# Sums of weight quadrants by accumulating transfers in a seven-product feed-forward block

## The chip, the core and the metric

One Trainium2 chip, one of its cores. TensorE multiplies, VectorE and ScalarE (ACT) work on tiles, GpSimd (POOL) does small work, SyncE (SP) issues transfers, and 16 DMA engines carry them. The metric is device time in microseconds (us) of one execution; lower is better.

## The reference, cut to what matters

One layer of a streaming encoder over 512 rows of 1024 features: a feed-forward block, a mixer with three kinds of attention, a second feed-forward block, a final norm. The change touches the two feed-forward blocks alone, which are of one form (`D_FF` is 2816, all in float32):

```python
def swiglu(h, wg, wu, wd):
    return (jax.nn.silu(h @ wg) * (h @ wu)) @ wd

x = x + 0.5 * swiglu(rmsnorm(x, ffn1_norm[l]), ffn1_wg[l], ffn1_wu[l], ffn1_wd[l])
...
x = x + 0.5 * swiglu(rmsnorm(x, ffn2_norm[l]), ffn2_wg[l], ffn2_wu[l], ffn2_wd[l])
```

## The kernel before

Every float32 product is made of three matmuls of split operands: a tile is split into a high part (a cast by ACT, line 77) and a low part (a subtraction by VectorE, line 78), and high x high, high x low and low x high are summed.

The up products of a feed-forward block are computed by a scheme with seven products of quarter size in place of eight (the Strassen-Winograd scheme). A pair of feature tiles is an `Item`; there are 11 per block, 22 in the kernel. Its weights are a 2 by 2 grid of quadrants of 128 x 1024 words (512 KB): quadrants 0 and 1 are the first feature tile with the first and the second half of the contraction, 2 and 3 the second feature tile with the same. In one quadrant the columns of gate and of up weights stand side by side. The moving operands are the matching seven matrices `M[1]` to `M[7]`, made once per block by `Operands.combine` (lines 205 to 231) from the transposed, normalised rows: `t1` to `t4` are sums of quarters of those, held in buffers from `quarter()`, and each is split into `M[5]`, `M[6]`, `M[7]`, `M[4]`.

`Item.prep(p)` (line 371) gives the weight block of product p. Products 1, 2 and 4 use a quadrant as it was loaded (`raw`, a buffer out of six under the tag `raw`, loaded by the SP queue at line 98). The other four use sums of quadrants, which VectorE makes: s1 (line 379, product 5), s2 (line 380, product 6), s4 (line 385, product 3) and s3 (line 389, product 7). Sums lie in `quarter()` buffers: two tags, `kx` and `w4`, taken in turn, two buffers each. A new block begins with `t1` to `t4` in all four of them, so its first sums take the buffers that those leave. `block` then splits the raw tile or sum into one of six slots (four `whi`/`wlo`, two `fhi`/`flo`).

`Item.run(p, blk)` (line 418) multiplies: 24 matmuls of 128 x 256 columns (`mm7`, line 354), into three PSUM banks: `y` (tag `s`, two buffers) collects products 1, 6, 7 and 4, `z` (tags `p` and `o` in turn) collects 5 and 3, product 2 has a bank of tag `g`. Between them `snap` (line 397) copies what `y` holds so far to SBUF by ACT, after products 1, 6 and 7; `plus` adds such a copy to another bank; `gated` (line 405) makes silu(gate) x up.

The jobs go through `run_jobs` (line 320), which calls `prep` up to six blocks ahead of `run`. The code lists an item's jobs as 6, 5, 7, the next item's 1, then 4, 3 and the next item's 2. A scheduler sets the order on every engine from this, by what is ready in its own simulation; on TensorE, parts of jobs can be mixed. The first block handles 4 feature tiles (two items), then three times 6 (three items) per feed-forward block; after each such chunk its down product is run (`wd`, lines 110 to 112), and its first job comes ahead of the last item's 4 and 3. The first chunk starts with 1 and 2 of both of its items.

Of the kernel before, what the change touches and what calls it, by code (L numbers as in the profile page):

```python
# [41 lines left out]
HS = S // 2  # L42
# [5 lines left out]
def layer_kernel(ctx: ExitStack, tc: tile.TileContext, a: dict, out: bass.AP):  # L48
# [128 lines left out]
    def quarter():  # L177

        quarters[0] += 1
        return base.tile([P, 1024], F32, tag=("w4", "kx")[quarters[0] % 2], name="quarter", bufs=2)  # L180
# [4 lines left out]
    class Operands:  # L185
# [18 lines left out]

        def combine(self, t):
            M, (r0, r1) = self.M, self.raw
            sub = nc.vector.tensor_tensor
            cols, first = slice(t * P, (t + 1) * P), slice(t % 2 * P, (t % 2 + 1) * P)

            def part(i, raw, c):  # L210
                split(raw, M[i][0][:, :, c], M[i][1][:, :, c])

            if t < 2:
                part(1, r0[:, :, cols], cols)
                part(2, r1[:, :, cols], cols)
                return
            if t == 2:
                self.t1, self.t2 = k4(quarter()), k4(quarter())
            t1, t2 = self.t1, self.t2
            sub(out=t1[:, :, first], in0=r0[:, :, cols], in1=r0[:, :, first], op=ALU.subtract)  # L220
            sub(out=t2[:, :, first], in0=r1[:, :, cols], in1=t1[:, :, first], op=ALU.subtract)
            part(6, t2[:, :, first], first)
            if t == 3:
                lo, hi = slice(0, HS), slice(HS, S)
                split(t1, *M[5])
                t3, t4 = k4(quarter()), k4(quarter())
                sub(out=t3, in0=r1[:, :, hi], in1=r0[:, :, hi], op=ALU.subtract)
                split(t3, *M[7])
                sub(out=t4, in0=r1[:, :, lo], in1=t2, op=ALU.subtract)
                split(t4, *M[4])  # L230
                split(r1[:, :, hi], *M[3])

# [99 lines left out]
    def ffn(pre, x_sb, M, fp, after, raws=None, before_last=None, after_half=None):  # L332
# [24 lines left out]
        class Item:  # L357


            def __init__(self, ft, G, g0, raws):  # L360
                self.ft, self.G, self.g0 = ft, G, g0
                self.raws = list(raws or [])
                self.pr = [None, None]

            def raw(self, i):
                while len(self.raws) <= i:
                    n = len(self.raws)
                    self.raws.append(load(w1[self.ft + n // 2, n % 2], 1024))
                return self.raws[i]

            def prep(self, p):
                add = nc.vector.tensor_tensor
                if p == 1:
                    return block(self.raw(0))
                if p == 2:
                    return block(self.raw(1))
                if p == 6:
                    self.s1, self.s2 = quarter(), quarter()
                    add(out=self.s1, in0=self.raw(2), in1=self.raw(3), op=ALU.add)
                    add(out=self.s2, in0=self.s1, in1=self.raw(0), op=ALU.subtract)  # L380
                    return block(self.s2)
                if p == 5:
                    got = block(self.s1)
                    self.s4 = quarter()
                    add(out=self.s4, in0=self.raw(1), in1=self.s2, op=ALU.subtract)
                    return got
                if p == 7:
                    s3 = quarter()
                    add(out=s3, in0=self.raw(0), in1=self.raw(2), op=ALU.subtract)
                    return block(s3)  # L390
                if p == 4:
                    return block(self.raw(3))
                return block(self.s4)

            def snap(self):
                v = fp.tile([P, 512], F32, tag="snap", name="snap", bufs=3)
# [5 lines left out]
                nc.vector.tensor_tensor(out=c, in0=ps, in1=v, op=ALU.add)  # L402
                return c

            def gated(self, c, f, th):

                if self.pr[f] is None:
                    self.pr[f] = fp.tile([P, S], F32, tag="pr", name="pr", bufs=3)
                    self.n = 0
                sg = fp.tile([P, HS], F32, tag="sg", name="sg", bufs=2)  # L410
                nc.scalar.activation(out=sg, in_=c[:, :HS], func=AF.Silu)
                pr, cols = self.pr[f], slice(th * HS, (th + 1) * HS)
                nc.vector.tensor_tensor(out=pr[:, cols], in0=sg, in1=c[:, HS:], op=ALU.mult)

            def done(self, f):
                split(self.pr[f], *(v[:, self.g0 + f, :] for v in self.G))
# [1 line left out]
            def run(self, p, blk):  # L418
                if p == 1:
                    self.y = bank("s")  # L420
                    mm7(self.y, blk, 1, True)
                    self.p1 = self.snap()
                elif p == 2:
                    x = bank("g")
                    mm7(x, blk, 2, True)
                    self.gated(self.plus(x, self.p1), 0, 0)
                elif p == 6:
                    mm7(self.y, blk, 6, False)
                    self.u2 = self.snap()
                elif p == 5:  # L430
                    self.z = bank("p" if self.ft // 2 % 2 else "o")
                    mm7(self.z, blk, 5, True)
                elif p == 7:
                    mm7(self.y, blk, 7, False)
                    self.u3 = self.snap()
                    self.gated(self.plus(self.z, self.u3), 1, 1)
                elif p == 4:
                    mm7(self.y, blk, 4, False)
                    self.gated(self.y, 1, 0)
                    self.done(1)  # L440
                else:
                    mm7(self.z, blk, 3, False)
                    self.gated(self.plus(self.z, self.u2), 0, 1)
                    self.done(0)
# [5 lines left out]
        for n, nf in enumerate(CHUNKS):  # L450
# [8 lines left out]
            else:  # L459
                order += [(items[0], 1), (items[0], 2)]  # L460
            for i, item in enumerate(items):
                order += [(item, 6), (item, 5), (item, 7)]
                if i + 1 < len(items) and not (ft == 0 and i == 0):
                    order += [(items[i + 1], 1)]
                if ft == 0 and i == 0:
                    order += [(item, 4), (item, 3)]
                elif i + 1 < len(items):
                    order += [(item, 4), (item, 3), (items[i + 1], 2)]
# [659 lines left out]
```

## Time and profile before

| | |
|---|---|
| median of 3 runs | 1273.12 us (1272.8 to 1274.1) |
| the profiled execution, its own time | 1273.05 us |
| its span in the profile | 1271.3 us |
| first feed-forward block | about 0 to 372 us |
| second feed-forward block | about 914 us to the end |
| busy: TensorE / VectorE / ACT / POOL | 97% / 66% / 47% / 8% |

Rows of the trace name an instruction by engine, line and operation, with what it writes and reads. PE is TensorE's matmul, PEld its weight load, which overlaps; DVE is VectorE; SPq is the SP queue that issues transfers. "Idle" is the time for which the engine stood still just before an instruction, and the arrow names what ended it. An engine's idle time costs something only where the chain of work that ends last passes through it. Matmuls are pipelined, so that each is shown longer (0.28 us) than the 0.114 us after which the next begins.

### The profile page before, as it was taken

To read this page: it belongs to the slowest core of one execution; us is meant where nothing else is said; L and a number is where in the kernel's file an instruction comes from. 1 tells how busy PE (TensorE), PEld (TensorE's weight loads), DVE (VectorE), ACT (ScalarE), POOL (GpSimd) and SP (SyncE) were. 2 spreads that over 40 slices of the span, in tenths; PEclk is the share of its full clock that TensorE was granted. 3 is DMA by queue.
4 is the path that set the end of the run, shared out by engine and by line. 5 is a ranking of instruction groups with operands and counts; after the bars stand their busy time and mean duration, and the time that the engine had idled before them with its cause. 6 is when DMAs were issued, how large, how long until landed. Compare 5 with 4: busy or idle time off the path is not lost.

```text
span 1271.3 us, 19657 instructions
## 1 busy us (share of the span) xinstructions
PE 1232.4 (97%) x7808; PEld 1116.9 (88%) x7808; DVE 842.8 (66%) x1377; ACT 596.8 (47%) x1115; POOL 107.1 (8%) x108
## 2 busy tenths in 40 slices
PE   7799999999998999999999999999979999999997
PEld 7789989989986799999999999888878998998996
DVE  7977667667564756766765565453697766766753
ACT  7535425435443446554555454443463452543543
POOL 1100000000000301111221121020000000000002
PEclk8899999999999899999999999999989999999999
DMA  5533324322334403321222320254133242342311
GB/s 215 174 108 116 115 71 128 113 91 101 116 118 130 109 28 108 88 67 58 88 87 70 89 83 31 75 159 160 34 127 122 76 133 91 101 129 73 130 35 67
DMA packets 53084, 127.57 MB, mean 100 GB/s; under 512 B 10112, under 2 KB 10624, under 8 KB 52992
## 3 DMA queue, kind: packets, MB, share of 16 engines
q1 hardware_dynamic: 52416, 125.27, 30.9%
q8 instruction: 61, 1.00, 0.3%
q10 hardware_dynamic: 576, 1.05, 0.2%
q14 instruction: 31, 0.25, 0.1%
HBM read 122.11 MB, written 4.19 MB: 99 GB/s over the span
## 4 chain that ended last, share of the span: by engine, by line
PE 90%; DVE 4%; DMA 2%; ACT 1%; POOL 1%; issue 1%; SPq 0%; POOLq 0%; ACTq 0%; DVEq 0%
PE ps_s L354 19%; PE ps_g L110 9%; PE ps_g L112 9%; PE ps_g L111 9%; PE ps_o L354 5%; PE ps_p L110 4%; PE ps_p L354 4%; PE ps_p L111 4%; PE ps_p L112 4%; PE ps_g L354 4%; PE ps_s L110 2%; PE ps_s L112 2%; PE ps_s L111 2%; PE ps_o L881 2%; PE ps_s L849 2%; PE ps_t L697 1%
## 5 line engine op out<-in xcount | busy, mean ns | idle before, releaser
L77 ACT CAST whi<-wraw 128x1024 fp32r<-128x1024 f32 (+1 forms) x120 | 119.0, 993 | 141.3 <-PE ps_s L354 68.6
L78 DVE TENSOR_TENSOR wlo<-wraw,whi 128x1024 fp32r<-128x1024 f32 (+1 forms) x120 | 137.9, 1151 | 65.6 <-ACT whi L77 64.6
L354 PE MATMUL ps_s<-mhi,whi 128*128 128x256 f32 x496 | 138.3, 279 | 2.3 <-ACT snap L397 2.0
L354 PE MATMUL ps_s<-mlo,whi 128*128 128x256 f32 x496 | 137.7, 278 | 0.0
L354 PE MATMUL ps_s<-mhi,wlo 128*128 128x256 f32 x496 | 136.8, 278 | 0.0
L77 ACT CAST whi<-quarter 128x1024 fp32r<-128x1024 f32 x54 | 56.7, 1051 | 91.8 <-PE ps_s L354 22.7
L354 PEld LDWEIGHTS ps_s<-mhi,whi 128*128 128x128 f32 x496 | 93.8, 189 | 4.1 <-ACT snap L397 2.8
L110 PE MATMUL ps_p<-whi,hh 128*128 128x384 f32 (+1 forms) x264 | 94.8, 359 | 0.0
L354 PEld LDWEIGHTS ps_s<-mlo,whi 128*128 128x128 f32 x496 | 93.7, 189 | 1.0 <-DVE mlo L78 0.2
L354 PEld LDWEIGHTS ps_s<-mhi,wlo 128*128 128x128 f32 x496 | 93.2, 189 | 0.0
L112 PE MATMUL ps_p<-whi,hl 128*128 128x384 f32 (+1 forms) x264 | 89.2, 338 | 0.0
L111 PE MATMUL ps_p<-wlo,hh 128*128 128x384 f32 (+1 forms) x264 | 89.2, 338 | 0.0
L78 DVE TENSOR_TENSOR wlo<-quarter,whi 128x1024 fp32r<-128x1024 f32 x54 | 65.9, 1221 | 24.5 <-ACT whi L77 24.5
L110 PE MATMUL ps_g<-hh,fh 128*128 128x512 f32 x192 | 78.4, 408 | 0.0
L112 PE MATMUL ps_g<-hh,fl 128*128 128x512 f32 x192 | 75.8, 395 | 0.0
L111 PE MATMUL ps_g<-hl,fh 128*128 128x512 f32 x192 | 75.7, 394 | 0.0
L834 DVE CAST kx<-ps_t 128x256 fp32r<-128x256 f32 x32 | 13.6, 425 | 83.7 <-PE ps_t L832 83.7
L121 POOL TENSOR_TENSOR rsh<-msh,mhalf 128x4 f32<-128x4 f32 x38 | 45.2, 1191 | 276.9 <-DVE msh L127 225.2
L78 DVE TENSOR_TENSOR fl<-wraw,fh 128x768 fp32r<-128x768 f32 x48 | 50.0, 1042 | 26.1 <-ACT fh L77 26.1
L77 ACT CAST fhi<-quarter 128x1024 fp32r<-128x1024 f32 x34 | 35.5, 1049 | 59.1 <-PE ps_s L354 16.4
L354 PE MATMUL ps_s<-mhi,fhi 128*128 128x256 f32 x208 | 59.2, 285 | 2.5 <-ACT fhi L77 2.5
L354 PE MATMUL ps_s<-mlo,fhi 128*128 128x256 f32 x208 | 58.9, 283 | 0.0
(376 smaller groups left out, 3662.8 us busy)
## 6 DMA issues: line engine op xcount, KB each, us to landing
wraw<-in_ffn_w SPq DMA_DIRECT2D x88, 512.0 KB, 4.0
wraw<-in_ffn_wd SPq DMA_DIRECT2D x44, 512.0 KB, 3.9
wraw<-in_w_u SPq DMA_DIRECT2D x32, 384.0 KB, 3.3
wraw<-in_w_gb SPq DMA_DIRECT2D x32, 384.0 KB, 3.0
wraw<-in_w_gf SPq DMA_DIRECT2D x16, 384.0 KB, 3.1
wraw<-in_w_mem_kv SPq DMA_DIRECT2D x8, 512.0 KB, 4.1
wraw<-in_w_out SPq DMA_DIRECT2D x8, 512.0 KB, 4.5
x_sb<-in_x SPq DMA_DIRECT2D x4, 512.0 KB, 7.0
```

The lines of the kernel that those rows point to most:

```text
L77: nc.scalar.copy(out=hi, in_=raw)
L78: (engine or nc.vector).tensor_tensor(out=lo, in0=raw, in1=f32(hi), op=ALU.subtract)
L110: nc.tensor.matmul(ps, lhsT=st[0], rhs=mv[0], start=first, stop=False)
L111: nc.tensor.matmul(ps, lhsT=st[0], rhs=mv[1], start=False, stop=False)
L112: return nc.tensor.matmul(ps, lhsT=st[1], rhs=mv[0], start=False, stop=last)
L121: nc.gpsimd.tensor_tensor(out=rs, in0=ms, in1=mhalf[:, :n], op=ALU.pow)
L354: nc.tensor.matmul(ps[:, c], lhsT=x, rhs=y, start=first and j + k + n == 0, stop=k == 3 and n == 2, skip_group_check=True)
L697: nc.tensor.transpose(ps[:, j * P:(j + 1) * P], pt[:, j * P:(j + 1) * P], ident)
L834: nc.vector.tensor_copy(out=un.kx[:, :, qs], in_=heads(p2[:, 0:256], 2))
L849: nc.tensor.matmul(out_, lhsT=q, rhs=k, start=j == 0, stop=j == 1)
L881: nc.tensor.matmul(o[:, vs], lhsT=pT[:, j * P:(j + 1) * P], rhs=un.v[:, j, vs], start=j == 0, stop=j == i)
```

## The change

It makes s1, s3 and s4 without VectorE: `total(i, j)` loads one quadrant into a `quarter()` buffer by the SP queue, and then a transfer issued by POOL adds the other quadrant to it on arrival (`accum_op=ALU.add`). s1 = quadrants 2 + 3 is made at the prep of product 1, s3 = 2 + 0 at that of product 2. At product 6 VectorE adds quadrant 0 to s1 in place, and after the split of that sum another accumulating transfer adds quadrant 1 to it: the sum of all four, for product 3. Quadrant 2 is no longer loaded as a `raw` tile. Since transfers only add, the differences of the scheme become sums: signs are turned in `t1`, `t2` and `t4`, all seven products then come with the other sign for the first feature row of the grid, and the second tile's gate takes a factor of -1 (the Silu's scale, and a scalar in the last multiply). An item's jobs are listed as 5, 6, 7 in place of 6, 5, 7.

```diff
-            sub(out=t1[:, :, first], in0=r0[:, :, cols], in1=r0[:, :, first], op=ALU.subtract)
-            sub(out=t2[:, :, first], in0=r1[:, :, cols], in1=t1[:, :, first], op=ALU.subtract)
+            sub(out=t1[:, :, first], in0=r0[:, :, first], in1=r0[:, :, cols], op=ALU.subtract)
+            neg(out=t2[:, :, first], in0=r1[:, :, cols], scalar=-1.0, in1=t1[:, :, first], op0=ALU.mult,
+                op1=ALU.subtract)
...
-                sub(out=t4, in0=r1[:, :, lo], in1=t2, op=ALU.subtract)
+                neg(out=t4, in0=r1[:, :, lo], scalar=-1.0, in1=t2, op0=ALU.mult, op1=ALU.subtract)
...
+            def total(self, i, j):
+
+                v = quarter()
+                nc.sync.dma_start(out=v, in_=self.quadrant(i))
+                nc.gpsimd.dma_start(out=v, in_=self.quadrant(j), accum_op=ALU.add)
+                return v
+
             def prep(self, p):
-                add = nc.vector.tensor_tensor
                 if p == 1:
+                    self.s1 = self.total(2, 3)
                     return block(self.raw(0))
                 if p == 2:
+                    self.s3 = self.total(2, 0)
                     return block(self.raw(1))
+                if p == 5:
+                    return block(self.s1)
                 if p == 6:
-                    self.s1, self.s2 = quarter(), quarter()
-                    add(out=self.s1, in0=self.raw(2), in1=self.raw(3), op=ALU.add)
-                    add(out=self.s2, in0=self.s1, in1=self.raw(0), op=ALU.subtract)
-                    return block(self.s2)
-                if p == 5:
+
+                    nc.vector.tensor_tensor(out=self.s1, in0=self.s1, in1=self.raw(0), op=ALU.add)
                     got = block(self.s1)
-                    self.s4 = quarter()
-                    add(out=self.s4, in0=self.raw(1), in1=self.s2, op=ALU.subtract)
+                    nc.gpsimd.dma_start(out=self.s1, in_=self.quadrant(1), accum_op=ALU.add)
                     return got
                 if p == 7:
-                    s3 = quarter()
-                    add(out=s3, in0=self.raw(0), in1=self.raw(2), op=ALU.subtract)
-                    return block(s3)
+                    return block(self.s3)
                 if p == 4:
                     return block(self.raw(3))
-                return block(self.s4)
+                return block(self.s1)
...
-                nc.scalar.activation(out=sg, in_=c[:, :HS], func=AF.Silu)
+                nc.scalar.activation(out=sg, in_=c[:, :HS], func=AF.Silu, scale=sign)
                 pr, cols = self.pr[f], slice(th * HS, (th + 1) * HS)
-                nc.vector.tensor_tensor(out=pr[:, cols], in0=sg, in1=c[:, HS:], op=ALU.mult)
+                nc.vector.scalar_tensor_tensor(out=pr[:, cols], in0=c[:, HS:], scalar=sign, in1=sg, op0=ALU.mult,
+                                               op1=ALU.mult)
...
-                order += [(item, 6), (item, 5), (item, 7)]
+                order += [(item, 5), (item, 6), (item, 7)]
```

## Rows read from the trace of the kernel before

**Rows 1.** The page, part 1: engines, busy us, share, instructions.
```profile
PE 1232.4 (97%) x7808; PEld 1116.9 (88%) x7808; DVE 842.8 (66%) x1377; ACT 596.8 (47%) x1115; POOL 107.1 (8%) x108
```

**Rows 2.** Stretches: length, PE, PEld, DVE, ACT, POOL busy, clock, DMA share, GB/s.
```profile
95.00:187.00 92.00, 92.00 (x650) 85.59 (x649) 63.56 (x74) 39.67 (x54) 0.00 (x0) 1.00 0.33 104
...
30.00:41.00 11.00, 4.52 (x21) 3.27 (x20) 10.56 (x15) 6.48 (x10) 4.60 (x1) 0.67 0.15 48
...
925.00:946.00 21.00, 14.53 (x99) 13.70 (x99) 21.00 (x23) 12.26 (x16) 0.00 (x0) 0.84 0.30 101
```

**Rows 3.** Waits of PE over the span: releaser, us in total, times, longest.
```profile
PE ps_o L354 <- ACT whi L77: 7.3, 2, 3.7
...
PE ps_g L354 <- ACT fhi L77: 3.0, 1, 3.0
...
PE ps_s L354 <- ACT snap L397: 2.0, 3, 0.7
```

**Rows 4.** The chain in order of time: start, us, what (an item near 100 us).
```profile
101.07 1.20 PE ps_o L354 x10
102.27 2.73 PE ps_s L354 x24
105.00 1.68 PE ps_o L354 x14
...
118.00 2.73 PE ps_o L354 x24
```

**Rows 5.** Groups by line, VectorE: count, busy us, mean ns, idle before (s1).
```profile
L379 DVE TENSOR_TENSOR quarter<-wraw 128x1024 f32<-128x1024 f32 x22 | 26.9, 1222 | 3.6 <-DMA wraw<-in_ffn_w 3.3
```

**Rows 6.** The timeline, POOL and VectorE, the first feed-forward block's start.
```profile
6.27 0.55 POOL L121 TENSOR_TENSOR rs<-ms,mhalf 128x1 f32<-128x1 f32 x1 [4.98 <-DVE ms L193]
...
28.93 1.22 DVE L78 TENSOR_TENSOR mlo<-quarter,mhi 128x1024 fp32r<-128x1024 f32 x1
...
30.42 4.60 POOL L121 TENSOR_TENSOR rs<-ms,mhalf 128x1 f32<-128x1 f32 x1 [10.18 <-DVE ms L156]
...
35.06 0.75 DVE L141 SCALAR_TENSOR_TENSOR xn<-mt,rs,gain 128x512 f32<-128x512 f32 x1 [0.44 <-POOL rs L121]
35.72 0.69 DVE L402 TENSOR_TENSOR cc<-ps_g,snap 128x512 f32<-128x512 f32 x1
...
39.25 1.22 DVE L78 TENSOR_TENSOR wlo<-quarter,whi 128x1024 fp32r<-128x1024 f32 x1
```

**Rows 7.** The timeline, VectorE and TensorE, the second feed-forward block's start.
```profile
924.23 4.09 DVE L78 TENSOR_TENSOR mlo<-quarter,mhi 128x1024 fp32r<-128x1024 f32 x4
...
933.37 1.22 DVE L78 TENSOR_TENSOR wlo<-quarter,whi 128x1024 fp32r<-128x1024 f32 x1
...
945.00 0.39 PE L354 MATMUL ps_s<-mhi,fhi 128*128 128x256 f32 x1 [0.28 <-ACT fhi L77]
...
945.95 0.39 PE L354 MATMUL ps_p<-mhi,fhi 128*128 128x256 f32 x1 [0.44 <-ACT fhi L77]
```

**Rows 8.** Transfers: the SP queue's total, and issues with us to landing.
```profile
q1 hardware_dynamic: 52416, 125.27, 30.9%
...
wraw<-in_ffn_w SPq DMA_DIRECT2D x88, 512.0 KB, 4.0
...
x_mid<-x_sb SPq DMA_DIRECT2D x4, 512.0 KB, 2.8
...
x_sb<-x_mid SPq DMA_DIRECT2D x4, 512.0 KB, 5.5
```

**Rows 9.** The timeline, TensorE after a `snap` between products 6 and 7.
```profile
48.43 0.19 PEld L354 LDWEIGHTS ps_s<-mhi,whi 128*128 128x128 f32 x1 [0.88 <-ACT snap L397]
48.43 0.39 PE L354 MATMUL ps_s<-mhi,whi 128*128 128x256 f32 x1 [0.68 <-ACT snap L397]
```

**Rows 10.** The timeline, ACT and VectorE, the block of product 6 near 101 us.
```profile
101.04 1.05 ACT L77 CAST whi<-quarter 128x1024 fp32r<-128x1024 f32 x1 [1.20 <-PE ps_g L354]
...
102.12 1.23 DVE L78 TENSOR_TENSOR wlo<-quarter,whi 128x1024 fp32r<-128x1024 f32 x1 [0.25 <-ACT whi L77]
```

More of the change, by code (lines that the diff above doesn't have):

```diff
@@ L206, in combine @@
             M, (r0, r1) = self.M, self.raw
-            sub = nc.vector.tensor_tensor
+            sub, neg = nc.vector.tensor_tensor, nc.vector.scalar_tensor_tensor
             cols, first = slice(t * P, (t + 1) * P), slice(t % 2 * P, (t % 2 + 1) * P)
@@ L361, in __init__, with quadrant @@
                 self.ft, self.G, self.g0 = ft, G, g0
-                self.raws = list(raws or [])
+                self.raws = dict(enumerate(raws or []))
                 self.pr = [None, None]
+            def quadrant(self, i):
+                return w1[self.ft + i // 2, i % 2]
             def raw(self, i):
-                while len(self.raws) <= i:
-                    n = len(self.raws)
-                    self.raws.append(load(w1[self.ft + n // 2, n % 2], 1024))
+                if i not in self.raws:
+                    self.raws[i] = load(self.quadrant(i), 1024)
                 return self.raws[i]
+            def total(self, i, j):
[3 more added lines that the diff above has]
+                return v
             def prep(self, p):
-                add = nc.vector.tensor_tensor
                 if p == 1:
+                    self.s1 = self.total(2, 3)
                     return block(self.raw(0))
                 if p == 2:
+                    self.s3 = self.total(2, 0)
                     return block(self.raw(1))
+                if p == 5:
+                    return block(self.s1)
                 if p == 6:
-                    self.s1, self.s2 = quarter(), quarter()
-                    add(out=self.s1, in0=self.raw(2), in1=self.raw(3), op=ALU.add)
-                    add(out=self.s2, in0=self.s1, in1=self.raw(0), op=ALU.subtract)
-                    return block(self.s2)
-                if p == 5:
+                    nc.vector.tensor_tensor(out=self.s1, in0=self.s1, in1=self.raw(0), op=ALU.add)
                     got = block(self.s1)
-                    self.s4 = quarter()
-                    add(out=self.s4, in0=self.raw(1), in1=self.s2, op=ALU.subtract)
+                    nc.gpsimd.dma_start(out=self.s1, in_=self.quadrant(1), accum_op=ALU.add)
                     return got
                 if p == 7:
-                    s3 = quarter()
-                    add(out=s3, in0=self.raw(0), in1=self.raw(2), op=ALU.subtract)
-                    return block(s3)
+                    return block(self.s3)
                 if p == 4:
                     return block(self.raw(3))
-                return block(self.s4)
+                return block(self.s1)
             def snap(self):
@@ L403, in plus, with gated @@
                 return c
-            def gated(self, c, f, th):
+            def gated(self, c, f, th, sign=1.0):
                 if self.pr[f] is None:
@@ L435, in run @@
                     self.u3 = self.snap()
-                    self.gated(self.plus(self.z, self.u3), 1, 1)
+                    self.gated(self.plus(self.z, self.u3), 1, 1, -1.0)
                 elif p == 4:
                     mm7(self.y, blk, 4, False)
-                    self.gated(self.y, 1, 0)
+                    self.gated(self.y, 1, 0, -1.0)
                     self.done(1)
```

## The prediction
> **What bounds the kernel now.** I read the page's first part, then busy time by stretch, then TensorE's waits, then the chain in order of time, then the starts of both feed-forward stages instruction by instruction. TensorE is busy 97% of the span, VectorE 66% and POOL 8% [rows 1]. All that is changed lies in the feed-forward stages. A chunk there (95 to 187 us) has TensorE busy for all 92.00 us at the full clock, VectorE for 63.56 [rows 2]. A product is 24 matmuls and takes 2.73 us [rows 4], so an item of seven takes 19.1 us. Three items and the 144 matmuls of the down product make up the chunk and leave nothing idle. Work taken off VectorE gives nothing back in such a chunk.
>
> Idle time of TensorE stands at the two starts, where the opposite holds: of 30 to 41 us it is busy for 4.52 of 11.00 us and VectorE for 10.56; of 925 to 946 us for 14.53 of 21.00, VectorE for all 21.00 [rows 2]. The waits say for what: 7.3 us over two waits of an `ps_o` product (the fifth) for the ACT copy of its block, 3.0 us of a `ps_g` one, 2.0 us in three waits for `snap` [rows 3]. So all that the change can win lies in some 13 us at two places, and the question is whether a sum made by transfers is there sooner than one that VectorE makes.
>
> **What is taken off VectorE.** Per item three of four adds go (s1, s3, s4); s2 stays. An add is 1222 ns, and there are 22 of each kind, one per item [rows 5], so 66 x 1.22 = 81 us of 842.8. In the chunks this is hidden under TensorE, value nothing; at the starts it is what could be gained.
>
> **What turning the signs costs.** The last multiply of each gate (88 of them) and three ops of `combine` become scalar_tensor_tensor. The nearest pair of rows is 128x512: 0.75 us in that form, 0.69 as tensor_tensor [rows 6]. For 256 columns that is 0.03 x 88 = 2.6 us of VectorE, hidden; at a start about 0.2 us stands on the path. The scale in the Silu changes no instruction: nothing.
>
> **What the order 5, 6, 7 costs.** Product 7 adds to the bank that 6 has just filled, and `snap` must read it between them; product 5 lay there before. The uncovered case is in the trace: the weight loads stand still for 0.88 us, the matmuls for 0.68 [rows 9]. (0.68 is counted from a matmul's modelled end; 0.88 is nearer to the loss.) It happens where nothing else is ready. Where something is, the order on TensorE is mixed: ten matmuls of a `ps_o` product, then 24 of `ps_s`, then the other 14 of `ps_o` [rows 4], although the code lists product 6 before 5. After 6 the next item's product 1 is mostly ready, with the other `s` bank. So I take nothing for it; uncovered it is a rival. At the two starts 5, 6, 7 was already the real order, with the stall in it [rows 9].
>
> **What the transfers cost.** Per item there were four loads of 512 KB; now there are five and three accumulating ones. An accumulating transfer and POOL as its issuer are not in the trace. Occupancy: the SP queue moved 125.27 MB in 30.9% of the span [rows 8], 393 us for 239 times 524 KB, or 1.64 us of all engines for each. Eight take 13.1 us of an item's 19.1. If an accumulating one counts twice, for it must read what it adds to, eleven take 18.0 us: full, but under the bound. The trace has no row that decides between the two. The Trainium skill (Collectives: The Full Stack, "Part 3: Why 7× under link rate") puts a reducing transfer at half the rate of a copy, since it reads two sources; by that the 18.0 us would hold, and no run here shows it.
>
> Latency is what matters at the starts. From below it is the fastest 512 KB row, 2.8 us; from above two median loads one after the other, 8.0 us. I take 5.5 us, the row of four loads in flight together [rows 8], since at a start several of these transfers run at once. Issuing on POOL: the small power op is the nearest row, 0.55 us with VectorE quiet, 4.60 us beside a VectorE without gaps [rows 6]. I take 0.55, since where it counts first, at 35 us, VectorE has a gap (it waits 0.44 us for POOL itself [rows 6]), and keep 4.60 as the other end. The Trainium skill (SBUF — State Buffer, "Who interferes with whom") says that a VectorE op with two SBUF inputs holds up POOL ops that read SBUF, with which the 4.60 agrees. It infers that writing descriptors is not held up by such ops, and by that 0.55 is the right end.
>
> **First start, 30 to 41 us.** s1 takes the buffer that t1 leaves, and t1 is last read by the op that ends at 28.93 + 1.22 = 30.15 us [rows 6]. Before, the add was next to follow, its operands long loaded. Now two transfers must follow instead. Load: 30.15 + 0.2 + 4.0 = 34.35. POOL is in its power op until 30.42 + 4.60 = 35.02, and the accumulating transfer is queued behind it. Issue and transfer: 35.02 + 0.55 + 5.5 = 41.1. ACT copy 1.05 [rows 10] and the low part 1.22 give 43.3; before, the low part of product 5 ended at 39.25 + 1.22 = 40.47 [rows 6]. Product 5 comes **2.9 us later**, and 6, 7, 4, 3 hang on it. (s3 is wanted two products, 5.5 us, later than s1 and its buffer, t2's, is free about as early: nothing of its own.) With 2.8 us for either transfer the difference is about +0.2, with 8.0 us +5.4.
>
> **Second start, 925 to 946 us.** t1 is the second of the four ops that begin at 924.23 [rows 7], so free at about 926.0. Load until 926.2 + 4.0 = 930.2, issue and transfer until 936.3, copy and low part until 938.5. Before: 933.37 + 1.22 = 934.6 [rows 7], so 3.9 us later. VectorE no longer stands behind its adds afterwards, which gives back at most the two small waits for copies around 945 us, 0.28 + 0.44 = 0.7 us [rows 7]: **3.2 us later**. With 2.8 us each: 0.7 us earlier; with 8.0 us: +5.7.
>
> **In the chunks.** s1 and s3 of an item have the second buffer of their tags and can be fetched an item ahead; the SP queue has three loads per item behind them in place of four. The tight one is s4: it may start once the low part of block 6 is made (102.12 + 1.23 = 103.35 [rows 10]) and must be landed 2.3 us before product 3 begins at 118.00 [rows 4], which leaves 12.4 us; 9.7 if the next item's product 2 runs after 3 instead of before. 5.5 + 0.55 fits, and so does 8.0 + 0.55. Nothing. If it were late, ACT's copy for product 3 would wait at the head of ACT's queue, with the next copies and a `snap` behind it, and TensorE behind those.
>
> **Sum.** 2.9 + 3.2 = 6.1 us on the profiled 1273.05 us (span 1271.3 and 1.75 around it; the median is 1273.12): **1279 us**, by the bounds of the transfers alone 1272.5 to 1284.
>
> **The rivals.** *Just in time, no change:* the transfers are as quick as the fastest row; the sums above give -0.5 us in all, 1272.5. For it: the queues are nearly idle at the starts (DMA share 0.15 and 0.30 [rows 2]). Against: four plain and four accumulating transfers want to run within some 10 us there.
>
> *Faster:* the VectorE-bound stretches shorten because six to eight adds leave them. It needs s1 before VectorE would have made it, which the buffers allow only with transfers under 2.8 us; then products 5 to 3 of both starts come some 2 us earlier each and the small waits go, 5 us in all: 1268. Against it stands that the chunks have nothing to give.
>
> *The snap uncovered:* if nothing fills the gap between 6 and 7, the 20 items that had cover pay 0.88 each, 17.6 us, with the starts 1297. For it: the code asks for this very order. Against it: the mixing in [rows 4].
>
> *s4 late, or the engines full:* it decides from 9.7 us for issue and landing. At the far ends, 4.60 + 8.0 = 12.6 us, product 3 is 2.9 us late in 20 items, 58 us, 1337; at one microsecond late it is 20 us, 1299. For it: 18.0 of 19.1 us of engine time if an addition reads twice.
>
> *That it does not do what it says:* the adds must leave VectorE, so only their place could fail, and this changes no time of its own.
>
> **How the numbers follow.** Forecast (1276 to 1286) 0.40; just in time 0.21; faster 0.14; snap 0.13; s4 late or engines full 0.12. Some 0.2%, 2.5 us, is what a measurement here can tell from no change. Faster 0.14, same 0.21, slower 0.65. The range from 1270 to 1300 holds the forecast, the unchanged case, the snap and the milder half of the late one; left out are most of the faster case and the far end of the late one.
>
> **What would show it.** Right: TensorE still without idle time in the chunks, VectorE near 760 us, the `ps_o` products of both starts waiting longer than 3.7 us, for a copy that itself waits for a transfer. Snap: some 20 more waits of TensorE for L397. Late s4: ACT waiting for a transfer before copies of `quarter` all through the chunks. I am wrong if the transfer from issue to landing is far from 5.5 us, or if the scheduler moves t1's last reader earlier.

## The result and the profile after

The changed kernel takes **1303.56 us** (median of four runs, 1300.57 to 1306.03), the kernel before 1273.61 in the same comparison: 1.0232 times the time, 95% interval 1.0207 to 1.0257. It is slower, as forecast, but by 30 us and not by 6. The profiled execution is 1303.72 us with a span of 1301.9, which is 30.6 more than the span of before.

First the page of after: busy time of the engines, the busy share of the DMA engines over the 40 slices, and the queues (packets, MB, share of 16 engines).

```profile
PE 1242.2 (95%) x7808; PEld 1123.6 (86%) x7808; DVE 772.2 (59%) x1311; ACT 596.8 (46%) x1115; POOL 162.8 (13%) x174
...
DMA  6985656836533422312221220254097674693521
...
q1 hardware_dynamic: 55584, 136.80, 32.0%
q0 software_dynamic: 9504, 34.61, 15.4%
```

VectorE is relieved by 70.6 us (842.8 to 772.2, [rows 1]), where 81 less 2.6 were worked out, and TensorE stands still for longer: 1301.9 less 1242.2 is 59.7 us, before it was 38.9. The other 9.8 us are longer busy time of the same 7808 matmuls; the mean granted clock over the span is 0.976 where it was 0.987. The queue q0 is new; it carries the 66 accumulating transfers, and its row gives their price. 15.4% of 1301.9 us over 66 is 3.04 us of all 16 engines for one. The 261 transfers of 524 KB that q1's 136.80 MB amount to took 32.0%, so 1.60 us each.

The transfers of after: issuing queue, count, KB, median us from issue to landing. The first row is the same load as in [rows 8], where it was 4.0.

```profile
wraw<-in_ffn_w SPq DMA_DIRECT2D x66, 512.0 KB, 4.6
quarter<-in_ffn_w POOLq DMA_DIRECT2D x66, 512.0 KB, 6.5
quarter<-in_ffn_w SPq DMA_DIRECT2D x44, 512.0 KB, 5.5
```

The waits of TensorE (what, releaser, us in total, times, longest), beside [rows 3]:

```profile
PE ps_o L358 <- ACT fhi L77: 13.7, 4, 6.8
PE ps_s L358 <- ACT snap L407: 7.2, 5, 2.3
PE ps_g L358 <- ACT fhi L77: 5.8, 2, 3.0
```

Product 5 still waits for its block at both starts, 6.8 and 5.4 us where the two waits of before were 7.3 together (the other two of the four in the first row, 0.8 and 0.7 us, stand in the second chunks). `snap` stands for 7.2 us where it was 2.0.

Where the time went is read from the starts of each chunk's first up product. The table gives the us from one such start to the next (the first column from the span's start, the last to its end; FFN 1 and 2 are the two feed-forward blocks). Its rows below the second belong to the experiments.

| kernel | FFN 1: first chunk | second | third | last chunk and what follows | FFN 2: first chunk | second | third | rest |
|---|---|---|---|---|---|---|---|---|
| before | 95.45 | 91.87 | 91.39 | 634.85 | 75.62 | 91.87 | 91.39 | 98.86 |
| after | 105.52 | 98.49 | 92.01 | 635.87 | 84.21 | 94.88 | 91.97 | 98.95 |
| e1, signs and order | 98.29 | 91.84 | 91.97 | 635.57 | 75.99 | 91.96 | 91.97 | 98.81 |
| e6, signs | 96.41 | 91.87 | 91.39 | 634.67 | 75.68 | 91.87 | 91.39 | 98.82 |
| e3, starts by VectorE | 98.02 | 95.85 | 92.01 | 636.34 | 77.02 | 96.29 | 91.97 | 99.20 |
| e4, plain transfers | 98.64 | 91.84 | 91.97 | 636.97 | 81.84 | 91.84 | 91.97 | 99.03 |
| e5, POOL in order | 104.97 | 91.83 | 91.98 | 635.85 | 85.07 | 91.84 | 91.97 | 98.99 |
| e2, s4 by VectorE | 102.63 | 91.84 | 92.02 | 636.40 | 83.80 | 91.84 | 92.02 | 98.95 |
| e7, s1 early | 106.79 | 95.94 | 91.96 | 636.26 | 83.74 | 96.18 | 92.01 | 99.02 |
| e8, e3 and e5 | 98.39 | 91.84 | 91.97 | 636.48 | 77.10 | 91.84 | 92.02 | 99.26 |
| e10, before with one sum by transfer | 97.31 | 91.87 | 91.39 | 635.92 | 76.24 | 91.87 | 91.39 | 99.21 |

After less before: +10.1, +6.6, +0.6, +1.0, +8.6, +3.0, +0.6, +0.1, together 30.6. So the two starts pay (18.7), the two second chunks (9.6), and the rest together 2.3. Each row is one execution. The second and third chunks repeat within 0.1 us where nothing was changed in them; the first column does not: e6, whose median cannot be told from that of before, has 0.96 us more there. So differences of about 1 us in it are not read as effects, nor are those in the column that holds the mixer.

**The first start.** Timeline of after: start and duration in us, engine, instruction, in brackets the idle time before it and what ended that.

```profile
31.00 3.66 SPq L380 DMA_DIRECT2D quarter<-in_ffn_w  x3
31.24 3.46 POOL L121 TENSOR_TENSOR rs<-ms,mhalf 128x1 f32<-128x1 f32 x1 [11.04 <-DVE ms L156]
35.20 1.04 POOL L381 DMA_DIRECT2D quarter<-in_ffn_w  x1 [0.50 <-issue]
43.67 1.04 ACT L77 CAST fhi<-quarter 128x1024 fp32r<-128x1024 f32 x1 [7.13 <-DMA quarter<-in_ffn_w]
44.75 1.23 DVE L78 TENSOR_TENSOR flo<-quarter,fhi 128x1024 fp32r<-128x1024 f32 x1 [6.53 <-ACT fhi L77]
44.77 0.58 PE L358 MATMUL ps_o<-mhi,fhi 128*128 128x256 f32 x1 [6.79 <-ACT fhi L77]
...
51.02 0.87 POOL L397 DMA_DIRECT2D quarter<-in_ffn_w  x1
61.46 1.99 ACT L77 CAST whi<-quarter 128x1024 fp32r<-128x1024 f32 x2 [5.00 <-DMA quarter<-in_ffn_w]
64.31 0.58 ACT L407 COPY snap<-ps_s 128x512 f32<-128x512 f32 x1
64.94 0.39 PE L358 MATMUL ps_s<-mhi,whi 128*128 128x256 f32 x1 [2.27 <-ACT snap L407]
```

The sequence is the predicted one up to the issue: t1's buffer is free near 31 us, the loads go out, POOL ends its power op at 34.70, and the addition for s1 is issued at 35.20 (forecast 35.02). Then it takes until 43.67, 8.5 us, where I had put 0.55 + 5.5. The low part of block 5 ends at 45.98, 5.5 us later than before, where 2.9 was forecast. While s1's addition is under way, two more additions and four loads are in flight with it. And it goes on: s4's addition, issued at 51.02, keeps ACT idle for 5.00 us. In ACT's queue `snap` stands behind that copy, and TensorE behind `snap`.

Stretches of after, columns as in [rows 2]:

```profile
41.00:52.00 11.00, 6.64 (x37) 6.14 (x38) 6.47 (x8) 6.16 (x9) 2.55 (x4) 0.62 1.03 289
52.00:66.00 14.00, 11.29 (x95) 10.88 (x94) 7.96 (x8) 6.39 (x9) 1.74 (x2) 1.00 0.92 226
118.00:146.00 28.00, 24.42 (x195) 23.93 (x195) 15.34 (x19) 11.06 (x17) 2.81 (x4) 0.92 0.63 156
...
66.00:80.00 14.00, 12.49 (x93) 12.21 (x92) 10.43 (x15) 7.28 (x13) 1.75 (x2) 0.88 1.04 321
...
296.00:362.00 66.00, 66.00 (x524) 63.93 (x523) 39.07 (x46) 31.56 (x44) 3.49 (x4) 1.00 0.57 148
```

From 41 to 80 us the DMA share (the last but one number) is 0.92 to 1.04: the engines have no room left. The sums of two items, the raw quarters and the down weights all go through them there. In a later chunk (296 to 362 us) the share is 0.57 and TensorE is busy for all 66.00 us.

**The second chunk.** Timeline of after at the place in FFN 1's second chunk that pays most; it is about the s4 of one item.

```profile
120.52 1.23 DVE L78 TENSOR_TENSOR wlo<-quarter,whi 128x1024 fp32r<-128x1024 f32 x1 [0.25 <-ACT whi L77]
121.77 0.33 SPq L380 DMA_DIRECT2D quarter<-in_ffn_w  x1
129.80 0.86 POOL L381 DMA_DIRECT2D quarter<-in_ffn_w  x1 [8.95 <-DMA quarter<-in_ffn_w]
130.34 1.22 POOL L397 DMA_DIRECT2D quarter<-in_ffn_w  x1
139.28 1.04 ACT L77 CAST whi<-quarter 128x1024 fp32r<-128x1024 f32 x1 [7.82 <-DMA quarter<-in_ffn_w]
141.84 0.58 PE L358 MATMUL ps_g<-mhi,fhi 128*128 128x256 f32 x1 [2.82 <-ACT fhi L77]
```

Block 6 is made at 121.75, so s4's addition (L397) may go from then on. It goes at 130.34. Ahead of it in POOL's queue stands a later item's addition (L381), and that one waits 8.95 us for its own load, which SP had only issued at 121.77. s4 lands near 139.2, ACT has stood for 7.82 us, and TensorE stands for 2.82, for the copy that comes behind s4's in ACT's queue.

This stretch (118 to 146 us) has TensorE idle for 3.58 of 28.00 us, all the idle time of a chunk that is 6.6 us longer. The other 3 us go with the granted clock: its mean is 0.92 in the stretch, so for a part of it TensorE ran at 1.2 and not at 2.4 GHz; in the same chunk of e5 below, without the standstill, it is 1.00. Likewise 0.88 for 66 to 80 us, behind the standstill at 64.94, and 0.62 for 41 to 52. A wait of TensorE costs here more than its length.

### The profile page after: what moved, and what is told of

Its sections match the earlier page's. It is cut to its first block, busy times and chain, and to the rows that moved or that the text cites. A ratio compares the mean times of both kernels' runs of the same rounds, so it can differ in the third digit from the quotient of the medians.

```text
span 1301.9 us, 19817 instructions
## 1 busy us (share of the span) xinstructions
PE 1242.2 (95%) x7808; PEld 1123.6 (86%) x7808; DVE 772.2 (59%) x1311; ACT 596.8 (46%) x1115; POOL 162.8 (13%) x174
## 3 DMA queue, kind: packets, MB, share of 16 engines
q1 hardware_dynamic: 55584, 136.80, 32.0%
q0 software_dynamic: 9504, 34.61, 15.4%
## 4 chain that ended last, share of the span: by engine, by line
PE 84%; DMA 7%; DVE 4%; ACT 2%; issue 2%; POOL 1%; SPq 0%; POOLq 0%; ACTq 0%; DVEq 0%
PE ps_s L358 16%; PE ps_g L110 9%; PE ps_g L112 9%; PE ps_g L111 9%; DMA quarter<-in_ffn_w 5%; PE ps_o L358 5%; PE ps_p L110 4%; PE ps_p L112 4%; PE ps_p L111 4%; PE ps_g L358 4%; PE ps_p L358 3%; PE ps_s L110 2%; PE ps_s L112 2%; PE ps_s L111 2%; PE ps_o L892 2%
## 5 line engine op out<-in xcount | busy, mean ns | idle before, releaser
L358 PE MATMUL ps_s<-mhi,whi 128*128 128x256 f32 x512 | 144.9, 283 | 7.5 <-ACT snap L407 7.2
L358 PE MATMUL ps_s<-mhi,wlo 128*128 128x256 f32 x512 | 144.0, 281 | 0.1
L358 PE MATMUL ps_s<-mlo,whi 128*128 128x256 f32 x512 | 144.1, 281 | 0.0
L358 PEld LDWEIGHTS ps_s<-mhi,whi 128*128 128x128 f32 x512 | 98.5, 192 | 9.4 <-ACT snap L407 8.2
L358 PEld LDWEIGHTS ps_s<-mlo,whi 128*128 128x128 f32 x512 | 98.4, 192 | 1.0 <-DVE mlo L78 0.2
L358 PEld LDWEIGHTS ps_s<-mhi,wlo 128*128 128x128 f32 x512 | 98.4, 192 | 0.4 <-DVE wlo L78 0.3
L381 POOL DMA_DIRECT2D quarter<-in_ffn_w x44 | 38.6, 878 | 301.8 <-DMA quarter<-in_ffn_w 176.8
L78 DVE TENSOR_TENSOR flo<-quarter,fhi 128x1024 fp32r<-128x1024 f32 x34 | 41.5, 1222 | 52.2 <-ACT fhi L77 52.2
```

Of the source, the lines that this page charges most:

```text
L78: (engine or nc.vector).tensor_tensor(out=lo, in0=raw, in1=f32(hi), op=ALU.subtract)
L358: nc.tensor.matmul(ps[:, c], lhsT=x, rhs=y, start=first and j + k + n == 0, stop=k == 3 and n == 2, skip_group_check=True)
L381: nc.gpsimd.dma_start(out=v, in_=self.quadrant(j), accum_op=ALU.add)
```

## The experiments

My theory after the result, **A**: all 30 us come from the transfers. At the starts the sums by transfer come late and fill the engines (18.7 us); in the second chunks POOL's queue holds s4 back behind a later item's addition (9.6). Its rivals have letters in the texts on record: the new order (B), or the signs and not the order (S); the backlog that a start leaves for the second chunk (C); transfers that are slow, not their place on POOL (D); the chain of load, wait and second transfer, whether it adds or not (E); engines that are full at the starts, and not the buffer that comes free late (F). The kernel before ran at 1273.15 to 1273.53 us beside them.

**e1: signs and order alone.** All sums go back to VectorE, the new signs and the order stay:

```
-                    self.s1 = self.total(2, 3)
...
-                    self.s3 = self.total(2, 0)
...
+                    self.s1 = quarter()
+                    add(out=self.s1, in0=self.raw(2), in1=self.raw(3), op=ALU.add)
...
-                    nc.gpsimd.dma_start(out=self.s1, in_=self.quadrant(1), accum_op=ALU.add)
+                    self.s4 = quarter()
+                    add(out=self.s4, in0=self.raw(1), in1=self.s2, op=ALU.add)
...
+                    s3 = quarter()
+                    add(out=s3, in0=self.raw(0), in1=self.raw(2), op=ALU.add)
```

> All four sums by VectorE again, with the turned signs and the order 5, 6, 7 kept: what the change does apart from its transfers. Theory A (all 30 us come from the transfers: engines full at the two starts, and POOL's queue in the second chunks): 1274 us, within 3 us of the kernel before, no TensorE wait for a snap in the chunks. Rival B (part of the loss is the order, product 7 right behind 6 with the snap between them): 0.88 us for each of the 20 items that had cover, up to 1291 us.

Measured 1277.9, ratio 1.0037 (1.0024 to 1.005): theory A misses here, since 4.7 us are not the transfers', and rival B has a part, not the 17.6 us that it could have had. TensorE's waits in its first 100 us, and one of the `snap` waits in the timeline:

```profile
PE ps_o L358 <- ACT fhi L77: 5.0, 1, 5.0
PE ps_s L358 <- ACT snap L411: 2.7, 3, 1.5
...
66.25 0.38 PE L358 MATMUL ps_s<-mhi,whi 128*128 128x256 f32 x1 [1.55 <-ACT snap L411]
```

Before had 3.6 us for product 5's block there and 1.4 for `snap`; the two waits rise by 2.7, and the first start is 2.8 longer. The rest is 0.6 us in each third chunk, 0.7 ahead of the second block and 0.4 at its start.

**e6: the signs alone.** As e1, with the old order:

```
-                order += [(item, 5), (item, 6), (item, 7)]
+                order += [(item, 6), (item, 5), (item, 7)]
```

> Sums by VectorE with the turned signs, but in the old order 6, 5, 7. With 5, 6, 7 the same kernel was 0.37% (some 4.7 us) over the kernel before, 2.8 us of it in the first start and 0.6 us in each later chunk. Theory B2 (the order does that): 1273.5 us, chunks of 91.4 us again. Rival S (the longer forms of the last multiply and of the combining ops do it): 1277 to 1278 us, chunks of 92.0 us.

Measured 1273.97, ratio 1.0003 (0.9994 to 1.0012). So the signs cost nothing that can be measured (rival S falls), and of e1's 4.7 us some 4 are the **order's**. Beside e6, e1's first start is 1.9 us longer, and 1.55 of that is the wait at 66.25. It stands in the second item: before and e6 run product 5's matmuls between those of 6 and 7 there (60.83 to 63.47 us in before), and e1 runs 7 right behind 6, with the `snap` bare between them. In the chunks that did not come about: between 95 and 280 us TensorE shows no wait at all in before, e6 and e1. A third chunk is 0.6 us longer without a wait because matmuls begin further apart: in e1's, 140 of those with blocks in `whi` and `wlo`, from 195.8 to 212.3 us, come every 117.8 ns on average, in before's third chunk such matmuls come every 113.5. 140 times 4.3 ns is 0.6 us. Why they come further apart no run shows.

**e3: the starts by VectorE.** The two items of each block's first chunk use e1's `prep`, all others the transfers:

```
             def prep(self, p):
+                return self.prep_vector(p) if self.ft < CHUNKS[0] else self.prep_dma(p)
```

> The two items of the first chunk of each feed-forward block take their sums from VectorE as before, all other items by transfers as in the changed kernel. From the stretches: the first chunks of the changed kernel take 10.1 and 8.6 us longer than before, the second ones 6.6 and 3.0 us. Theory A (a start loses because the sums can't be loaded before t1 to t4 leave their buffers and because the engines are then full): the 18.7 us of the two first chunks come back, 1285 us, with the second chunks still some 10 us long. Rival C (the backlog of transfers that a start leaves behind is what makes the second chunk late, too): the second chunks recover as well, 1275 us.

Measured 1288.12, ratio 1.0123 (1.0104 to 1.0142). The starts are near e1's lengths (98.02 to 98.29; 77.02 to 75.99): what they lost beyond e1 was due to the sums by transfer in their own items, some 15 us. The second chunks stay 4.0 and 4.4 us too long, so the backlog of a start (C) is not what makes them late.

**e5: POOL in order.** A later item's additions for s1 and s3 may not stand ahead of s4's on POOL:

```
+                ins = nc.gpsimd.dma_start(out=v, in_=self.quadrant(j), accum_op=ALU.add)
+                if last_s4[0] is not None:
+                    tc.add_manual_dep(ins.ins, last_s4[0].ins.name, ..., reason="POOL order")
```

> The changed kernel with one more rule: on POOL, the accumulating transfers of s1 and s3 of a later item come after that of s4 of the item before, so that s4 is never queued behind an addition that waits for its load. Theory A: in the second chunks (6.6 and 3.0 us too long) the wait of ACT for s4 goes, and some 2 us of the first chunks' loss, 1293 us. Rival D (s4 is late because transfers are slow, not because of its place in POOL's queue): 1303 us, with ACT still waiting 7 to 8 us for a transfer in the second chunk.

Measured 1293.64, ratio 1.016 (1.0138 to 1.0182). The second chunk of FFN 1 as a stretch, and POOL in it:

```profile
105.00:196.80 91.80, 91.80 (x649) 85.41 (x648) 54.87 (x65) 39.59 (x54) 8.00 (x9) 1.00 0.63 170
...
125.56 0.88 POOL L402 DMA_DIRECT2D quarter<-in_ffn_w  x1 [22.44 <-DVE flo L78]
126.16 2.06 POOL L382 DMA_DIRECT2D quarter<-in_ffn_w  x2
```

TensorE is busy for all 91.80 us. s4's addition (here L402) leaves first, and the two of a later item (L382) behind it. Both second chunks are at 91.84, so 9.4 us of span go with nothing but the order on POOL. Rival D, slow transfers, asked for 1303 us and falls.

**e2: s4 by VectorE**, in place, s1 and s3 by transfers:

```
-                    nc.gpsimd.dma_start(out=self.s1, in_=self.quadrant(1), accum_op=ALU.add)
+                    nc.vector.tensor_tensor(out=self.s1, in0=self.s1, in1=self.raw(1), op=ALU.add)
```

> s1 and s3 by transfers, s4 by VectorE (quadrant 1 is added in place from its loaded tile): seven transfers per item, two of them additions. Theory A: no addition is queued on POOL behind another item's load, so the second chunks take 91.9 us; the first chunks lose some 2 us less each, since two of six additions per start are gone: 1290 us. Rival D (lateness comes from s1 and s3 themselves): second chunks still 3 to 6 us too long, 1300 us.

Measured 1290.53, ratio 1.0132 (1.0116 to 1.0149). The second chunks are whole again by this road too, though a later item's addition still waits on POOL: nothing urgent stands behind it any more. The first start gets 2.9 us back as well: product 5 starts 1.1 us sooner than in after (43.67), and the wait of 2.27 us behind s4's copy in the timeline above is not there. How the 2.9 us divide this run does not show.

**e4: the same transfers without the addition.** POOL's three per item overwrite:

```
-                nc.gpsimd.dma_start(out=v, in_=self.quadrant(j), accum_op=ALU.add)
+                nc.gpsimd.dma_start(out=v, in_=self.quadrant(j))
...
```

> The three transfers that POOL issues write over what is there and do not add to it (so s1, s3 and s4 lack what they should add to); waits, queues and byte counts in HBM stay. Theory A (an addition costs the engines twice a plain transfer, 3.04 against 1.60 us of all 16, and this fills them at the starts): these transfers land in 4 to 5 us in place of 6.5, and about half of the 30 us come back, 1288 us. Rival E (the chain load, wait, POOL, second transfer is what costs, whatever the second one does): over 1298 us.

Measured 1285.94, ratio 1.0101 (1.0086 to 1.0116). Its queue q0, its transfers, a stretch of its first start, POOL in FFN 1's second chunk, and ACT at the second start:

```profile
q0 software_dynamic: 9504, 34.61, 8.0%
...
quarter<-in_ffn_w POOLq DMA_DIRECT2D x66, 512.0 KB, 4.6
...
52.00:66.00 14.00, 14.00 (x123) 14.00 (x123) 10.65 (x12) 9.12 (x12) 1.58 (x3) 1.00 0.92 344
...
120.55 0.53 POOL L381 DMA_DIRECT2D quarter<-in_ffn_w  x1 [8.62 <-DMA quarter<-in_ffn_w]
121.10 0.54 POOL L397 DMA_DIRECT2D quarter<-in_ffn_w  x1
...
943.01 1.04 ACT L77 CAST fhi<-quarter 128x1024 fp32r<-128x1024 f32 x1 [6.66 <-DMA quarter<-in_ffn_w]
```

The same packets and bytes, and 8.0% of 1284.1 us over 66 is 1.56 us each. The **addition itself** thus costs 3.04 less 1.56, 1.48 us of all engines, and 1.9 us to landing (6.5 to 4.6). Without it the first start loses 3.2 us, little beyond e1's 2.8, so there it is the addition that costs: at the same DMA share of 0.92, the stretch of 52 to 66 us moves 344 GB/s where it was 226. Rival E asked for over 1298 us and falls as a whole, but it has a part at the second start, which still loses 6.2: s1's plain transfer, issued at 935.43, takes 7.6 us beside the loads (the DMA share of 933 to 947 us is 0.90), ACT waits 6.66 us for it, and TensorE 4.6 us for product 5's block. The second chunks are at 91.84 with nothing done about POOL's order: s4 still leaves only 6.2 us after its block is made (114.87 to 121.10), behind a transfer that waited 8.62 us for its load, but it lands 4.6 us later and in time. So the 9.6 us need both, the queue and the price.

**e7: a buffer that is free early.** If t1's buffer were the trouble, and not full engines (F), the first item's s1 in a buffer of its own should help:

```
-                v = quarter()
+                v = buf4k("sraw") if self.ft == 0 and j == 3 else quarter()
```

> The changed kernel, but s1 of the first item of each feed-forward block is built in a buffer that is free long before (one of the raw ones), so its load does not wait for t1. Theory A, part 1 (the buffer that t1 leaves late, and the chain of two transfers after it, set the start): product 5 starts at 41 us or before in the first block and some 10 us earlier in the second; 4 to 6 us come back, 1298 us. Rival F (the engines, full at the starts, set it: s3 and s4 are just as late): product 5 earlier, but 7 and 3 wait in its place, under 2 us back, 1302 us.

Measured 1305.19, ratio 1.0248 (1.0228 to 1.0267): no gain, as rival F had it; after itself is at 1.0232. Wait, timeline and stretch of its first start:

```profile
PE ps_s L358 <- ACT snap L407: 15.6, 4, 9.1
...
14.71 1.03 POOL L381 DMA_DIRECT2D sraw<-in_ffn_w  x1
...
46.63 1.04 ACT L77 CAST whi<-quarter 128x1024 fp32r<-128x1024 f32 x1 [9.33 <-DMA quarter<-in_ffn_w]
49.48 0.58 ACT L407 COPY snap<-ps_s 128x512 f32<-128x512 f32 x1
...
41.00:52.00 11.00, 1.90 (x9) 1.90 (x10) 3.94 (x4) 4.94 (x7) 0.87 (x1) 0.69 1.02 260
```

s1's addition now leaves at 14.71 us, and product 5 doesn't stand for it any more. Its place is taken by s3: ACT waits 9.33 us for that transfer at the head of its queue, `snap` stands behind, and TensorE waits 9.1 us for `snap`. The engines are at 1.02. The buffer of s1 alone isn't what binds: the next sum is late in its place. Of s3's own lateness the run shows two parts and doesn't weigh them: its load could go only at 32.25 us, when VectorE was through with one of t1 to t4, and its addition then took 10.7 us (35.87 to 46.61). My sum for the start, which let s3 come along with "nothing of its own", has its fault here.

**e8: e3 and e5 together.**

> Both remedies: the first chunk of each block takes its sums from VectorE, and on POOL a later item's s1 and s3 come after s4. Theory A: nothing of the transfers' loss is left, and what stays over the kernel before is what the order alone costs (4.7 us): 1278 us, second chunks of 91.9 us. Rival G (two thirds of the items with eight transfers still lose some time each): 1282 us or more.

Measured 1280.06, ratio 1.0053 (1.0038 to 1.0068). That lies between theory A's 1278 and the 1282 of rival G (items with eight transfers lose some time each) and decides for neither. Of 30.6 us of span 23.0 are gone, and what is left is e1's 5.1 and 2.5 more, 2.0 of them ahead of the second block and at its start. In this version 18 of 22 items have their sums by transfers. The 12 of them in the second and third chunks show no loss and no gain: these chunks are as long as those of e1.

**e10: the kernel before with one sum by transfer.** Was there anything to win at the starts? Old signs and order, and only the first item's s1 of each block is loaded and added early, into a buffer of its own:

```
+                    if self.ft == 0:
+                        self.s1 = buf4k("sraw")
+                        nc.sync.dma_start(out=self.s1, in_=w1[1, 0])
+                        nc.gpsimd.dma_start(out=self.s1, in_=w1[1, 1], accum_op=ALU.add)
```

> The kernel before, old signs and old order, with one sum in each feed-forward block made by transfers: s1 of the first item is a load and an accumulating transfer into a buffer of its own, issued with the item's first product, long before the sum is wanted; all other sums stay with VectorE. Theory A (the transfers lose in the kernel after by buffers that come free late, by engines that they fill and by POOL's queue): here none of the three holds, so the addition lands in 5.5 to 6.5 us, product 5 of the first item does not wait for it, and VectorE has one add of 1.22 us less at either start. 1271 to 1273, with the first start up to 1.2 us shorter. Rival I (an accumulating transfer costs by itself, whoever waits for it: the engines it takes make the loads around it later): either start 1 to 3 us longer, 1275 to 1279, with ACT waiting for loads of the first two items.

Measured 1278.21, ratio 1.0035 (1.0021 to 1.0049): theory A missed, and by its number the rival (I: the addition makes the loads around it late) is right. Its mechanism does not show: the load from `in_ffn_w` lands in 3.9 us in the median (4.0 before), and at the first start ACT waits for no load of the first two items. TensorE, VectorE and ACT at the first start:

```profile
30.55 0.28 PE L354 MATMUL ps_o<-mhi,whi 128*128 128x256 f32 x1
...
36.66 1.21 DVE L386 TENSOR_TENSOR quarter<-sraw,wraw 128x1024 f32<-128x1024 f32 x1
...
38.86 0.63 ACT L137 ACTIVATE sq<-mt 128x512 f32<-128x512 f32 x1 [1.67 <-DMA mt<-in_mem]
...
39.49 1.03 ACT L77 CAST fhi<-quarter 128x1024 fp32r<-128x1024 f32 x1
...
40.57 0.58 PE L354 MATMUL ps_s<-mhi,fhi 128*128 128x256 f32 x1 [4.59 <-ACT fhi L77]
...
41.53 1.21 DVE L78 TENSOR_TENSOR flo<-quarter,fhi 128x1024 fp32r<-128x1024 f32 x1
```

The starts of products 5 and 6 in before:

```profile
34.66 0.58 PE L354 MATMUL ps_o<-mhi,whi 128*128 128x256 f32 x1 [3.64 <-ACT whi L77]
...
40.47 0.58 PE L354 MATMUL ps_s<-mhi,fhi 128*128 128x256 f32 x1 [2.17 <-ACT fhi L77]
```

Product 5 starts at 30.55 without a wait, in before at 34.66 after one of 3.64. But product 6 starts no sooner, at 40.57 where it was 40.47. Its block is made from s2, which VectorE has ready at 37.87, and the copy of it stands in ACT's queue behind work on the mixer's rows, which waits 1.67 us for their load. Most of product 5's matmuls came behind that point in before (41.06 to 45.01) and covered the wait for the low part of block 6; here they are through by then. Product 7 begins at 47.96 us, in before at 48.43 [rows 9]. An s1 that is there over 10 us sooner is worth half a microsecond at this point. The chunk is 1.9 us longer in the end: from 52 us on TensorE is idle for 2.8 us where it was 0.9, in waits for ACT and VectorE. How much of that is the transfer and how much another mixture of the products on TensorE, this run doesn't separate; nor does it explain the 1.1 us ahead of the second block.

No version beats the kernel before.

## Why the prediction was wrong, point by point

The sign was right and so were the places of the starts. The time missed the range by 3.6 us. Of the 30.6 us of span 6.1 were forecast. Of the other 24.5, some 9.6 are s4's in the second chunks and some 5 are what e1 keeps, most of it the order's, both priced at nothing; the rest is the transfers at the starts, which cost some 15 us and not 6.1. By its steps:

- **"Work taken off VectorE gives nothing back in such a chunk."** Right: VectorE went to 772.2 us (760 forecast), and the third chunks have 92.01 and 91.97 us, as in e1 (91.97 and 91.97), no gain.
- **Turning the signs: 0.2 us at a start.** Not contradicted: e6's median is 0.6 us over before, with an interval from -0.8 to 1.5, too wide to tell 0.2 from nothing.
- **"So I take nothing" for the order 5, 6, 7.** Wrong by some 4 us (e1, e6). The snap rival asked 0.88 for each of 20 items and is wrong as well (5 waits in place of 3, not 20 more). I had argued that at the two starts 5, 6, 7 "was already the real order". At the first start that holds for the first item alone: the second ran 6, 5, 7, and without product 5 in between, product 7 waits 1.55 us for `snap`. Another 1.2 us are the third chunks.
- **Engine time of an addition, 13.1 to 18.0 us per item.** The upper end is near: 3.04 us where twice 1.64 would be 3.28, so five loads and three additions take 17.1 us. The engines are full only where items crowd, at the starts. The Trainium skill (Collectives: The Full Stack, "Part 3: Why 7× under link rate") puts a reducing transfer at half the rate of a copy, since it reads two sources. The runs agree, with 3.04 against e4's 1.56 us.
- **Accumulating transfer 5.5 us, load 4.0, issue 0.55.** Mis-sized: 6.5 in the median and 8.5 with its issue for the one that counts (35.20 to 43.67), loads 4.6 and 5.5, issue 0.87. I had taken the row of four loads in flight as the crowded case. At the start the share is about 1.0, and three additions that cost double, with four loads beside them, are more than four loads. The upper end, 8.0 for the addition with 4.0 for the load, was near (+5.4 and +5.7 against the 5.5 and 6.6 of the next point); the sum should have used it there. As to POOL, L381's issues last 0.858 to 1.036 us through all the stages, while the small power op takes 3.46 at 31.24: so the 4.60 end did not come about. The 0.55 would have been right for a plain transfer: e4's take 0.53. The Trainium skill (SBUF — State Buffer, "Who interferes with whom") infers that VectorE's ops with two SBUF inputs do not hold up the writing of descriptors. The trace agrees, with at most 1.04 us for an L381 issue beside a busy VectorE.
- **First start 2.9, second 3.2.** The mechanism is right (product 5 waits for a copy that waits for the transfer), the size isn't: block 5 is 5.5 and 6.6 us later, and s3 and s4 behind it are late too. The starts lost 10.1 and 8.6, of which e1, without transfers, has 2.8 and 0.4. I followed one sum to its product and let the others come along; e7 shows that with s1 out of the way s3 takes its place, and e3 that some 15 us go when the sums at the starts are VectorE's again.
- **s4 in the chunks: "5.5 + 0.55 fits", nothing.** This is the step that failed in kind. The 12.4 us were right as a slack, and issue and landing alone would have fit (8.9 us from 130.34 to 139.2). What I left out is what stands **ahead of s4 on POOL**: 8.6 us passed before it was issued, and with the order on POOL fixed (e5) the 9.6 us of the two second chunks are gone. I had asked what queue a new wait holds up (ACT's, rightly) but not what the new transfer itself has to wait behind. The rival "s4 late" had the picture, and the wrong cause and place: it asked for every item, and it came in the two second chunks, 9.6 us. That a standstill also takes the clock with it was in none of my sums, though [rows 2] had the starts at 0.67 and 0.84.
- **Just in time, and faster.** Neither came about; in e10 even an s1 that never waits gave nothing at the first start.

What stays open: why matmuls come further apart in a third chunk under the new order; the 1.0 us ahead of the second block (e1 0.7, e4 2.1, e8 1.6, e6 none), for which TensorE's waits name no single cause and which one execution each hardly tells from nothing; and how the lateness of s3 at a start divides between its buffer and the full engines.

## What to carry to other kernels

A sum made by an accumulating transfer is not a load with a free addition: count it twice in engine time, give it the landing time of a crowded stretch where several fall together, and ask whether the engine that it relieves is what the kernel waits for. For each transfer that goes to another engine's queue, list what may stand ahead of it there and what that waits for; one edit that fixes that order gave back 9.4 us here. When the sum on one path is made earlier, follow the next one on the same path before counting a gain.

## What the runs showed of the hardware that was not expected

- The addition costs 1.48 us of all 16 engines for 512 KB (3.04 against 1.56 for the same bytes and packets without it), and 1.9 us of the median time to landing (6.5 against 4.6).
- A transfer that waits for its data holds the whole of POOL's queue: 8.95 us of waiting at L381, behind which a transfer stood that had been ready for 8.6.
- POOL's issue of an accumulating transfer took 0.86 to 1.04 us at L381, VectorE busy or not, and 0.87 to 1.23 at L397, where the three longest began while another was being issued; a plain one (e4) took 0.53. POOL's small vector op beside a busy VectorE took 3.46.
- Matmuls of one shape, with no wait between them and at the full clock, came every 113.5 ns in one stretch and every 117.8 in another (before and e1, third chunk); what sets the pace no run shows.
